# Rotary embedding and score matmul: the first batch in groups of eight heads, two row slots per step

## Chip, cores and metric

The kernel runs on one core of a Trainium2 chip. The metric is the device time of one execution in microseconds (us); the median of three runs before the change is 792.87 (792.67 to 793.26).

The engines of the core: TensorE (PE; its weight loads are shown as PEld) multiplies and transposes, VectorE (DVE) and ScalarE (ACT) work on elements and copy results out of the accumulator memory, GpSimd (POOL) and SyncE (SP) issue transfers. The transfers themselves run on 16 DMA engines.

## The reference

Sixteen batches, 512 rows, 16 heads of 64 elements, all float32. q and k are rotated by position, then for each row s every head h is multiplied with the same head of every row t; there is no scaling and no softmax.

```python
batch, seq, heads, dim = 16, 512, 16, 64
...
q_rot = concatenate([q1 * cos - q2 * sin, q1 * sin + q2 * cos], axis=-1)
k_rot = concatenate([k1 * cos - k2 * sin, k1 * sin + k2 * cos], axis=-1)
scores = np.einsum('bshd,bthd->bsht', q_rot, k_rot)
```

q and k are 33.6 MB each, the output is 268.4 MB.

## The kernel before

**Tiling.** The 512 rows of a batch are split into 128 partitions with C = 4 rows each: partition p holds rows 4p to 4p + 3, and the four places are called slots. A step i computes one slot of one batch for all 16 heads: i // 4 is the batch, i % 4 the slot, 64 steps in all. Each step has eight score steps p (`scores(i, p, st)`): one pair of heads each, two score matmuls of 64 x 128 by 64 x 512 into a score buffer `ps` (three buffers), and one copy by ScalarE (line 208) into the stage tile `st`, 128 partitions by 16 heads by 512. A full `st` is stored with one transfer of 4 MB, 32 KB in each partition.

**Rotation and transposes.** `rope` returns two lists of VectorE work, products (lines 149 and 150) and sums (line 154), on the loaded tile in place, with a scratch tile `part`. `transposed` turns four blocks of 128 x 128 into one bank `bank` (two buffers) by TensorE (line 170) and copies them with VectorE or ScalarE (line 185) into `qT` (two buffers) or `kT` (two buffers). `tr_act` does that for both halves, with ScalarE.

**The first batch** is done otherwise. Its q and k are cut by heads, not by slots: a unit n (0 to 3) is four heads of all 512 rows. The units are loaded into one tile `early`: first unit 0 of k and q (512 KB each), then units 1 to 3 in one transfer each (1536 KB each). `rope(which, n)` with n below 4 turns a unit; from 4 on, n names a slot of a later batch: `("k", 4)` is slot 0 of batch 1, `("q", 8)` would be slot 0 of batch 2. In the first batch step i computes unit i, that is four heads for all four slots: score step p has slot c = p // 2 and head pair hp = p % 2. After every second score step 1 MB is stored, four heads by 512 columns, 8 KB in each partition (line 211). Between the score steps stand, in each of the four steps, the next unit's rotation and transposes, and one slot of batch 1's k.

**Order.** All of it is under a hand-written schedule: each engine runs its instructions in the order in which the program issues them, and waits where an operand or a buffer is not ready. So an instruction that waits holds up all that is behind it on its engine. Stores and most loads are issued by SP, in order; a few loads later in the kernel go over GpSimd (`load_around`).

**Buffers.** The stage pool has three slots of 4 MB; `early` lies in one of them during the first batch. A step's `st` takes the slot of three steps before, and ScalarE's first copy into it waits until the stores from it have landed. By the trace step 2 takes the slot of step 0, step 3 that of `early`, step 4 that of step 1. Loaded tiles of later batches (`k_sb`, `q_sb`) have two buffers each; batch 1 and batch 2 fill them.

**The steady part** (line 264 on): in step i, q of step i + 1 is transposed after score steps 1 and 3 and copied by VectorE, k of the step four further after score steps 5 and 6 and copied by ScalarE; VectorE turns q two steps ahead and k five ahead.

Of the kernel before, what the change touches and what calls it, by code (L numbers as in the profile page):

```python
# [10 lines left out]
def kernel(  # L11
# [8 lines left out]
    nc = tc.nc  # L20
    fp32 = mybir.dt.float32
# [3 lines left out]
    B, S, H, D = q.shape  # L25
    HD = D // 2
    P = 128
    C = S // P
    HP = H // 2
    NST = B * C  # L30
    G = H // C
# [22 lines left out]

    st_first = [stage_pool.tile([P, H, S], fp32, tag="stage", name="st") for _ in range(2)]
    early = stage_pool.tile([P, 2 * C * H * D], fp32, tag="stage", name="early")
    units = {}
    used = [0]  # L60

# [51 lines left out]
    def load(which, b):  # L113

        if b >= B:
            return
        t = in_pool.tile([P, C, H * D], fp32, tag=which + "_in", name=which + "_sb")
        batches[which, b] = t
        if (which, b) in RELIEVED:
            load_around(which, b, t)  # L120
        else:
            nc.sync.dma_start(t.rearrange("p c (h d) -> p c h d", h=H), dram[which][b])
# [35 lines left out]
    kT = {}  # L158
    qT = {}

    def transposed(which, n, g, copy):


        bank = ps_t_pool.tile([P, 4, P], fp32, tag="ps_t", name="bank")
        for x in range(4):
            if n < C:
                src = units[which, n][:, x, P * g : P * (g + 1)]
            else:
                src = batches[which, n // C][:, n % C, P * (4 * g + x) : P * (4 * g + x + 1)]
            nc.tensor.transpose(bank[:, x, :], src, ident)  # L170
        src = bank
        if which == "q":
            if n not in qT:
                qT[n] = qt_pool.tile([P, HP, P], fp32, tag="qT", name="qT_t")
            dst = qT[n][:, 4 * g : 4 * g + 4, :]
        else:
            b = n // C
            if b not in kT:
                kT[b] = kt_pool.tile([P, HP, S], fp32, tag="kT", name="kT_t")
            if n < C:  # L180
                dst = kT[b][:, 2 * n + g].rearrange("p (t c) -> p t c", c=C)
                src = bank.rearrange("p c t -> p t c")
            else:
                dst = kT[b][:, 4 * g : 4 * g + 4, P * (n % C) : P * (n % C + 1)]
        copy(out=dst, in_=src)  # L185

    def store(i, st):
        nc.sync.dma_start(o_v[i // C, i % C], st)

    def scores(i, p, st):  # L190

        ps = ps_s_pool.tile([P, 2, S], fp32, tag="ps_s", name="ps")
        b = i // C
        if b == 0:
            c, hp = divmod(p, 2)
            lhs, rhs = qT[i][:, C * hp + c], kT[0][:, 2 * i + hp]
        else:
            lhs, rhs = qT[i][:, p], kT[b][:, p]
        for r in range(2):
            po, rh = ps[:, r, :], rhs[64 * r : 64 * r + 64, :]  # L200
            nc.tensor.matmul(  # L201
                out=po, lhsT=lhs[64 * r : 64 * r + 64, :], rhs=rh, start=True, stop=True
            )
        so, si = st[:, 2 * p : 2 * p + 2, :], ps
        if b > 0:
            so = so.rearrange("s r (t c) -> s r t c", c=C)
            si = si.rearrange("s r (c t) -> s r t c", c=C)
        nc.scalar.copy(out=so, in_=si)  # L208
        if b == 0 and p % 2 == 1:
            c = p // 2  # L210
            nc.sync.dma_start(o_v[0, c, :, G * i : G * (i + 1)], st[:, G * c : G * (c + 1)])
        elif b > 0 and p == HP - 1:
            store(i, st)

    def tr_act(which, n):
        for g in range(2):
            transposed(which, n, g, nc.scalar.copy)

    def run(ops):
        for op in ops:  # L220
            op()

    with tc.manual_schedule():
        for t, src in ((cos_t, cos), (sin_t, sin)):
            nc.scalar.dma_start(t, src.rearrange("(p c) j -> p c j", c=C))
        for head, heads in ((0, G), (G, H - G)):
            load_units("k", head, heads)
            load_units("q", head, heads)
        load("k", 1)
        load("q", 1)  # L230
        make_identity(nc, ident)
        nc.scalar.copy(out=ss_t[:, :, 0, :], in_=sin_t)
        nc.scalar.mul(ss_t[:, :, 1, :], sin_t, -1.0)
        for which in ("k", "q"):
            run(rope(which, 0))
            tr_act(which, 0)


        for i in range(C):
            st = st_first[i] if i < 2 else stage_pool.tile([P, H, S], fp32, tag="stage", name="st")  # L240
            if i < C - 1:
                dve = rope("k", i + 1) + rope("q", i + 1) + rope("k", C + i)
                nxt = [("k", i + 1), ("q", i + 1)]
            else:
                dve = rope("q", C) + rope("k", C + i) + rope("q", C + 1) + rope("k", 2 * C)
                nxt = [("q", C), ("k", C + i)]
            for p in range(HP):
                scores(i, p, st)
                if p in (0, 1) and i > 0:
                    run(dve[:1])  # L250
                    dve = dve[1:]
                    transposed("k", C + i - 1, p, nc.vector.tensor_copy)
                if p == 3 and i < 2:
                    load("kq"[i], 2)
                if p in (2, 6):
                    m = len(dve) - (4 if p == 2 else 2) - (2 if i == C - 1 else 0)
                    run(dve[:m])
                    dve = dve[m:]
                    tr_act(*nxt.pop(0))
            run(dve)  # L260
        load("k", 3)


        for i in range(C, NST):
            tr = {}
            if i + 1 < NST:
                tr[1], tr[3] = ("q", i + 1, 0), ("q", i + 1, 1)
            if i + C < NST:
                tr[5], tr[6] = ("k", i + C, 0), ("k", i + C, 1)
            dve = []  # L270
            if i + 2 < NST:
                dve += rope("q", i + 2)
            if i + 1 + C < NST:
                dve += rope("k", i + 1 + C)
            st = stage_pool.tile([P, H, S], fp32, tag="stage", name="st")
            for p in range(HP):
                scores(i, p, st)
                if p not in tr:
                    continue
                if tr[p][0] == "q":  # L280
                    run(dve[:1])
                    dve = dve[1:]
                    transposed(*tr[p], nc.vector.tensor_copy)
                else:
                    transposed(*tr[p], nc.scalar.copy)
            run(dve)
            if i % C == C - 2:
                load("q", i // C + 2)
            elif i % C == C - 1:
                load("k", i // C + 3)  # L290
# [30 lines left out]
```

## Time and profile before

| what | value |
|---|---|
| median of three runs | 792.87 us |
| profiled execution: first to last instruction (span) | 790.4 us |
| TensorE / VectorE / ScalarE / GpSimd busy | 684.4 / 544.7 / 562.0 / 11.9 us |
| DMA mean rate, bytes | 425 GB/s, 336.18 MB |
| share of SP's DMA queue in the 16 engines' span | 96.4% |
| stores of 4096 KB | 60, 24.7 us from issue to landing |
| stores of 1024 KB (first batch) | 16, 13.8 us from issue to landing |
| mean granted TensorE clock | 0.934 |

The profiled execution has no time of its own beside its span; the span is 2.5 us under the median of the runs.

How to read the profile: it shows one execution. Columns of a timeline are start (us from the span's start), duration, engine, line, operation, result and operand; in square brackets stands the idle time of the engine just before, and what ended it. "PEclk" is the granted TensorE clock. "x3" merges three instructions. A window lists the busy time of each engine with its number of instructions, and at the end the clock, the DMA engines' mean busy share and GB/s. The trace also holds a record of each DMA packet (queue, size, start, duration) and of each landing, where each of the 16 DMA engines raises a semaphore by one.

The first transfers are issued in this order, by the SP queue's timeline: the four loads of units at 0.74, 1.46, 2.11 and 2.78, batch 1's k at 3.45 and q at 4.17, the first two stores at 19.52 and 22.46, batch 2's k at 22.85, further stores, batch 2's q at 33.73, the sixteenth store at 62.29, batch 3's k at 62.72.

### The profile page before, as it was taken

How to read it: one execution, taken by the hardware profiler on the slowest of the kernel's cores; microseconds unless marked ns; L12 is line 12 of the kernel's file. 1: busy time of each engine (PE TensorE's matmuls, PEld its weight loads, DVE VectorE, ACT ScalarE, POOL GpSimd, SP SyncE). 2: the span in 40 equal slices, each digit the busy share in tenths (PEclk: the TensorE clock that was granted, in tenths of full speed). 3: DMA queues.
4: the chain of work that ended last, by engine and by line, in shares of the span. 5: the costliest groups of instructions: out<-in, count | busy, mean ns of one | idle time of the engine just before them, and what ended most of it. 6: DMA issues, size and time to landing. Idle time of an engine off the chain costs nothing.

```text
span 790.4 us, 7750 instructions
## 1 busy us (share of the span) xinstructions
PE 684.4 (87%) x3072; PEld 296.4 (38%) x3072; DVE 544.7 (69%) x516; ACT 562.0 (71%) x647; POOL 11.9 (2%) x24
## 2 busy tenths in 40 slices
PE   4989998988988889798996989889899798799960
PEld 2444443433433334343342433334334343344420
DVE  6999988666766678576785767667678487587400
ACT  3888886865857768486785866777577586588770
POOL 0000000000001000000000001000000000000000
PEclk9999999998999999898998989999899899899995
DMA  9999999999999999999999999999999999999997
GB/s 357 417 425 439 429 430 435 425 435 436 429 429 428 413 432 419 433 423 438 433 427 436 426 432 429 422 432 424 430 432 427 436 429 432 430 432 434 432 429 340
DMA packets 18836, 336.18 MB, mean 425 GB/s; under 512 B 2312, under 2 KB 3592, under 8 KB 4616
## 3 DMA queue, kind: packets, MB, share of 16 engines
q1 hardware_dynamic: 16704, 325.46, 96.4%
q0 software_dynamic: 1808, 10.10, 3.1%
q8 instruction: 24, 0.39, 0.2%
q10 hardware_dynamic: 288, 0.13, 0.1%
q14 instruction: 12, 0.10, 0.0%
HBM read 67.24 MB, written 268.44 MB: 425 GB/s over the span
## 4 chain that ended last, share of the span: by engine, by line
DMA 49%; PE 40%; ACT 5%; DVE 3%; issue 1%; ACTq 0%; SPq 0%; DVEq 0%
DMA out_dram<-st 46%; PE ps L201 30%; PE bank L170 10%; ACT st L208 5%; DMA q_sb<-in_q_dram 2%; DVE part L149 1%; DMA early<-in_k_dram 1%; DVE q_sb L150 0%; DVE k_sb L154 0%; DVE k_sb L150 0%; DVE q_sb L154 0%; DVE early L150 0%; DVE kT_t L185 0%; ACTq L316 0%; DVE early L154 0%
## 5 line engine op out<-in xcount | busy, mean ns | idle before, releaser
L208 ACT COPY st<-ps 128x1024 f32<-128x1024 f32 x512 | 495.7, 1020 | 192.6 <-DMA out_dram<-st 109.8
L201 PE MATMUL ps<-kT_t,qT_t 64*128 64x512 f32 x2048 | 544.0, 649 | 67.0 <-ACT st L208 67.0
L201 PEld LDWEIGHTS ps<-kT_t,qT_t 64*128 64x128 f32 x2048 | 183.6, 196 | 256.2 <-issue 133.3
L185 DVE COPY qT_t<-bank 128x512 f32<-128x512 f32 x118 | 81.6, 691 | 193.9 <-PE bank L170 193.9
L170 PEld LDWEIGHTS bank<-ident,q_sb 128*128 128x128 f32 x480 | 54.2, 149 | 99.0 <-issue 96.4
L170 PEld LDWEIGHTS bank<-ident,k_sb 128*128 128x128 f32 x480 | 50.3, 140 | 96.4 <-DVE k_sb L150 39.5
L170 PE MATMUL bank<-ident,q_sb 128*128 128x128 f32 x480 | 85.1, 304 | 0.9 <-PE ps L201 0.9
L170 PE MATMUL bank<-ident,k_sb 128*128 128x128 f32 x480 | 78.5, 286 | 1.6 <-DVE qT_t L185 1.2
L185 ACT COPY kT_t<-bank 128x512 f32<-128x512 f32 x122 | 72.4, 598 | 6.4 <-PE bank L170 6.4
L154 DVE TENSOR_TENSOR k_sb<-k_sb,part 128x1024 f32<-128x1024 f32 x60 | 73.5, 1225 | 2.1
L150 DVE TENSOR_TENSOR q_sb<-q_sb,cos_t 128x1024 f32<-128x1024 f32 x60 | 73.5, 1225 | 2.1
L150 DVE TENSOR_TENSOR k_sb<-k_sb,cos_t 128x1024 f32<-128x1024 f32 x60 | 73.5, 1225 | 2.0
L149 DVE TENSOR_TENSOR part<-q_sb,ss_t 128x1024 f32<-128x1024 f32 x60 | 73.5, 1225 | 2.0
L149 DVE TENSOR_TENSOR part<-k_sb,ss_t 128x1024 f32<-128x1024 f32 x60 | 73.0, 1216 | 0.9 <-DMA k_sb<-in_k_dram 0.7
L154 DVE TENSOR_TENSOR q_sb<-q_sb,part 128x1024 f32<-128x1024 f32 x60 | 72.9, 1216 | 0.0
L170 PE MATMUL bank<-ident,early 128*128 128x128 f32 x64 | 10.5, 315 | 12.4 <-DVE early L154 10.5
L170 PEld LDWEIGHTS bank<-ident,early 128*128 128x128 f32 x64 | 8.3, 161 | 17.4 <-issue 13.4
L149 DVE TENSOR_TENSOR part<-early,ss_t 128x1024 f32<-128x1024 f32 x8 | 9.8, 1222 | 5.8 <-DMA early<-in_k_dram 5.7
L98 POOL DMA_DIRECT2D q_sb<-in_q_dram x3 | 2.3, 752 | 620.2 <-PE bank L170 446.2
L154 DVE TENSOR_TENSOR early<-early,part 128x512 f32<-128x512 f32 x16 | 10.3, 687 | 0.2
L150 DVE TENSOR_TENSOR early<-early,cos_t 128x1024 f32<-128x1024 f32 x8 | 9.8, 1225 | 0.3
L185 ACT COPY qT_t<-bank 128x512 f32<-128x512 f32 x10 | 5.7, 629 | 3.2 <-PE bank L170 3.2
(12 smaller groups left out, 15.9 us busy)
## 6 DMA issues: line engine op xcount, KB each, us to landing
out_dram<-st SPq DMA_DIRECT2D x60, 4096.0 KB, 24.7
k_sb<-in_k_dram SPq DMA_DIRECT2D x13, 2048.0 KB, 28.3
q_sb<-in_q_dram SPq DMA_DIRECT2D x12, 2048.0 KB, 26.5
out_dram<-st SPq DMA_DIRECT2D x16, 1024.0 KB, 13.8
q_sb<-in_q_dram POOLq DMA_DIRECT2D x3, 1920.0 KB, 27.8
k_sb<-in_k_dram POOLq DMA_DIRECT2D x2, 1920.0 KB, 43.3
early<-in_k_dram SPq DMA_DIRECT2D x1, 1536.0 KB
early<-in_q_dram SPq DMA_DIRECT2D x1, 1536.0 KB
```

Source lines behind the costliest of these rows:

```text
L98: nc.gpsimd.dma_start(dst, src)
L149: nc.vector.tensor_tensor(pv, xs, ss, op=mult)
L150: nc.vector.tensor_tensor(xc, xc, cs, op=mult)
L154: nc.vector.tensor_tensor(y, y, z, op=add)
L170: nc.tensor.transpose(bank[:, x, :], src, ident)
L185: copy(out=dst, in_=src)
L201: nc.tensor.matmul(out=po, lhsT=lhs[64 * r : 64 * r + 64, :], rhs=rh, start=True, stop=True)
L208: nc.scalar.copy(out=so, in_=si)
```

## The change

Only the first batch is done in another order. A step i now computes two units (eight heads) for two slots: steps 0 and 1 take units 0 and 1 with slots 0, 1 and then 2, 3; steps 2 and 3 take units 2 and 3 likewise (`order`). Within a step the four score steps of the first unit come before the four of the second. A store is issued after score steps 5 and 7: eight heads by 512 columns of one slot, 2 MB, 16 KB in each partition; eight stores in place of sixteen. Batch 2's k is loaded ahead of all stores, right behind batch 1's loads, and batch 2's q after step 0. A table (`plan`) says after which score step which rotation, transpose or load is issued: VectorE turns units 0 to 3 of k and q one after the other, then batch 1's k slots 0 and 1, whose transposes it copies behind score steps 6 and 7 of step 2, and so on. In the list, "rope" is a rotation, "act" the transposes with ScalarE's copies, "dve" one half of a slot's transposes with VectorE's copy. `early` is allocated between the two first stage tiles. The steady part is as it was.

```diff
--- before.py
+++ after.py
@@ -54,8 +54,9 @@
 
 
 
-    st_first = [stage_pool.tile([P, H, S], fp32, tag="stage", name="st") for _ in range(2)]
+    st_first = [stage_pool.tile([P, H, S], fp32, tag="stage", name="st")]
     early = stage_pool.tile([P, 2 * C * H * D], fp32, tag="stage", name="early")
+    st_first.append(stage_pool.tile([P, H, S], fp32, tag="stage", name="st"))
     units = {}
     used = [0]
 
@@ -187,28 +188,37 @@
     def store(i, st):
         nc.sync.dma_start(o_v[i // C, i % C], st)
 
+    E8 = 2 * G
+    order = [
+        [(2 * (i // 2) + u, 2 * (i % 2) + c, hp) for u in range(2) for c in range(2) for hp in range(2)]
+        for i in range(C)
+    ]
+
     def scores(i, p, st):
 
         ps = ps_s_pool.tile([P, 2, S], fp32, tag="ps_s", name="ps")
         b = i // C
         if b == 0:
-            c, hp = divmod(p, 2)
-            lhs, rhs = qT[i][:, C * hp + c], kT[0][:, 2 * i + hp]
-        else:
-            lhs, rhs = qT[i][:, p], kT[b][:, p]
+            u, c, hp = order[i][p]
+            lhs, rhs = qT[u][:, C * hp + c], kT[0][:, 2 * u + hp]
+            at = E8 * (c % 2) + G * (u % 2) + 2 * hp
+        else:
+            lhs, rhs, at = qT[i][:, p], kT[b][:, p], 2 * p
         for r in range(2):
             po, rh = ps[:, r, :], rhs[64 * r : 64 * r + 64, :]
             nc.tensor.matmul(
                 out=po, lhsT=lhs[64 * r : 64 * r + 64, :], rhs=rh, start=True, stop=True
             )
-        so, si = st[:, 2 * p : 2 * p + 2, :], ps
+        so, si = st[:, at : at + 2, :], ps
         if b > 0:
             so = so.rearrange("s r (t c) -> s r t c", c=C)
             si = si.rearrange("s r (c t) -> s r t c", c=C)
         nc.scalar.copy(out=so, in_=si)
-        if b == 0 and p % 2 == 1:
-            c = p // 2
-            nc.sync.dma_start(o_v[0, c, :, G * i : G * (i + 1)], st[:, G * c : G * (c + 1)])
+        if b == 0 and u % 2 == 1 and hp == 1:
+            g = i // 2
+            nc.sync.dma_start(
+                o_v[0, c, :, E8 * g : E8 * (g + 1)], st[:, E8 * (c % 2) : E8 * (c % 2 + 1)]
+            )
         elif b > 0 and p == HP - 1:
             store(i, st)
 
@@ -228,6 +238,7 @@
             load_units("q", head, heads)
         load("k", 1)
         load("q", 1)
+        load("k", 2)
         make_identity(nc, ident)
         nc.scalar.copy(out=ss_t[:, :, 0, :], in_=sin_t)
         nc.scalar.mul(ss_t[:, :, 1, :], sin_t, -1.0)
@@ -236,28 +247,38 @@
             tr_act(which, 0)
 
 
+        plan = {
+            (0, 3): [
+                ("rope", "k", 1), ("act", "k", 1), ("rope", "q", 1), ("act", "q", 1),
+                ("rope", "k", 2), ("rope", "q", 2),
+            ],
+            (0, 7): [("load", "q", 2)],
+            (1, 2): [("act", "k", 2), ("rope", "k", 3), ("rope", "q", 3)],
+            (1, 6): [("act", "q", 2), ("rope", "k", C), ("rope", "k", C + 1)],
+            (2, 1): [("act", "k", 3)],
+            (2, 2): [("act", "q", 3)],
+            (2, 6): [("dve", "k", C, 0)],
+            (2, 7): [("dve", "k", C, 1), ("rope", "k", C + 2)],
+            (3, 1): [("dve", "k", C + 1, 0)],
+            (3, 2): [("dve", "k", C + 1, 1), ("rope", "q", C)],
+            (3, 4): [("dve", "k", C + 2, 0)],
+            (3, 5): [("dve", "k", C + 2, 1), ("rope", "k", C + 3)],
+            (3, 6): [("act", "q", C)],
+            (3, 7): [("act", "k", C + 3), ("rope", "q", C + 1), ("rope", "k", 2 * C)],
+        }
         for i in range(C):
             st = st_first[i] if i < 2 else stage_pool.tile([P, H, S], fp32, tag="stage", name="st")
-            if i < C - 1:
-                dve = rope("k", i + 1) + rope("q", i + 1) + rope("k", C + i)
-                nxt = [("k", i + 1), ("q", i + 1)]
-            else:
-                dve = rope("q", C) + rope("k", C + i) + rope("q", C + 1) + rope("k", 2 * C)
-                nxt = [("q", C), ("k", C + i)]
             for p in range(HP):
                 scores(i, p, st)
-                if p in (0, 1) and i > 0:
-                    run(dve[:1])
-                    dve = dve[1:]
-                    transposed("k", C + i - 1, p, nc.vector.tensor_copy)
-                if p == 3 and i < 2:
-                    load("kq"[i], 2)
-                if p in (2, 6):
-                    m = len(dve) - (4 if p == 2 else 2) - (2 if i == C - 1 else 0)
-                    run(dve[:m])
-                    dve = dve[m:]
-                    tr_act(*nxt.pop(0))
-            run(dve)
+                for what, which, n, *g in plan.get((i, p), ()):
+                    if what == "rope":
+                        run(rope(which, n))
+                    elif what == "load":
+                        load(which, n)
+                    elif what == "act":
+                        tr_act(which, n)
+                    else:
+                        transposed(which, n, g[0], nc.vector.tensor_copy)
         load("k", 3)
```

## The prediction

> **What bounds the kernel now.** I read the 40 slices and the table of DMA queues first.
>
> ```profile
> DMA  9999999999999999999999999999999999999997
> q1 hardware_dynamic: 16704, 325.46, 96.4%
> ```
>
> The 16 DMA engines are full in every slice but the last, while no compute engine is over 87%. So a microsecond in which they stand empty is lost for good, and one of packets that falls away is won. The windows say the same of the first 100 us.
>
> ```profile
> core 0: us, PE busy (x) PEld busy (x) DVE busy (x) ACT busy (x) POOL busy (x), PEclk, DMA share, GB/s
> 20.00:40.00 20.00, 20.00 (x105) 9.48 (x103) 19.40 (x21) 16.65 (x22) 0.00 (x0) 1.00 1.00 419
> 40.00:60.00 20.00, 17.91 (x93) 8.59 (x92) 19.62 (x22) 16.85 (x21) 0.00 (x0) 1.00 1.01 425
> 60.00:76.00 16.00, 14.75 (x72) 6.56 (x72) 15.66 (x15) 12.87 (x16) 0.00 (x0) 1.00 1.02 433
> ```
>
> But VectorE (DVE) is 97 to 98% busy here too: the first batch is where a second resource is nearly full. So I looked, in the timelines of ScalarE, VectorE and the SP queue, at what would make it late.
>
> ```profile
> 36.97 1.01 ACT L208 COPY st<-ps 128x1024 f32<-128x1024 f32 x1
> 40.59 1.93 ACT L208 COPY st<-ps 128x1024 f32<-128x1024 f32 x2 [2.61 <-DMA out_dram<-st]
> ...
> 44.85 1.29 DVE L154 TENSOR_TENSOR early<-early,part 128x512 f32<-128x512 f32 x2
> 46.18 1.22 DVE L149 TENSOR_TENSOR part<-k_sb,ss_t 128x1024 f32<-128x1024 f32 x1
> ...
> 66.02 1.23 DVE L149 TENSOR_TENSOR part<-q_sb,ss_t 128x1024 f32<-128x1024 f32 x1
> 67.27 1.23 DVE L150 TENSOR_TENSOR q_sb<-q_sb,cos_t 128x1024 f32<-128x1024 f32 x1
> 68.42 0.68 DVE L185 COPY qT_t<-bank 128x512 f32<-128x512 f32 x1
> ...
> 72.65 2.84 ACT L208 COPY st<-ps 128x1024 f32<-128x1024 f32 x3 [0.23 <-PE ps L201]
> ...
> 73.69 0.33 SPq L188 DMA_DIRECT2D out_dram<-st  x1
> ...
> 83.71 0.33 SPq L188 DMA_DIRECT2D out_dram<-st  x1
> ```
>
> The first two rows: step i = 2 writes into the stage slot of i = 0 and ScalarE stands until that slot's stores have landed (the last landing of the fourth is at 40.49 in the trace). VectorE does not feel it: it always has rotations queued that need nothing of that step, and from 5.67 to 66.02 its rows leave one hole, of 0.19. The last rows: q's products of i = 4, the copy at 68.42, and 5.27 us after its start the first 4 MB store, at 73.69. The next follows 10.02 later.
>
> How thin the DMA's reserve is there: the packet records of the trace have the first 32 KB packet, with which the first engine begins that store, at 77.3. From issue to first packet it takes 1.46 on SP's idle queue (issue at 0.74, packet at 2.2) and 0.96 on ScalarE's (0.74 to 1.7). So the store could have come only 77.3 - 73.69 - 1.46 = 2.15 us later before an engine ran dry.
>
> **The change, part by part.** *Packets.* Sixteen stores of 1 MB become eight of 2 MB. By the packet records an 8 KB packet takes 309 ns, a 16 KB one 611, the 4-byte packet that closes a store on each engine 9. Each engine had 16 x 8 = 128 of 8 KB and now has 64 of 16 KB: 64 x (618 - 611) = 0.45 us, and 8 x 9 = 0.07 for the closings: -0.52 us in all. [...]
>
> *The start.* VectorE turns k0, q0, k1, q1 in this order already, so q1 is done at 21.03 as now. The first store now needs six score steps and both units. Of TensorE and ScalarE I count from the rows of now: third score copy at 19.39, fourth 20.30, two bank copies of k1 (0.48 apart) to 22.3, q1's transposes once the two banks are free, its copies to 23.65, score steps five and six, whose copies end at 25.4 and 26.3. Store at 26.3 where the first was at 19.52; data at 27.8. The engines have k's load of batch 2 more to do by then: in the records the first 8 KB packet starts at 23.5, plus 8 x 0.611 = 4.9, gives 28.4. So no pause, by 0.6 us. That load and q's of batch 2 only change places with stores; both land long before their use. All later 2 MB stores of the batch (34.6, 37.5, about 48, 50, 58, 62.5 by the same counting) meet a queue that is 3 to 5 us ahead.
>
> *Step i = 2.* Its slot is again that of i = 0, whose two stores end where the four ended: 28.4 + 9.8 = 38.2 for the first engine against 38.3 now, so ScalarE starts at 40.5 again. What is queued behind it differs. VectorE, which waits for nothing, finishes k0 to k3 and q0 to q3 (8 rotations of 3.84 us, the distance from 5.67 to 9.52 in its timeline), then batch 1's slots 0 and 1 (3.78 each, 21.06 to 24.84): 5.67 + 30.72 + 7.56 = 43.95. Its next instruction is the copy of slot 0's transposes, and these stand on TensorE behind score step (2,6). That step needs the score buffer of (2,3), one of three, so ScalarE must first do 3 score copies at 0.905, two pairs of bank copies at 1.03 and the copy of (2,3), 1.01: 40.5 + 2.7 + 2.1 + 1.0 = 46.3. TensorE then takes 0.95 to the transposes and VectorE starts 0.69 after them (26.82 to 27.51 now): 47.9. **VectorE stands 4.0 us**, and about 1.0 more until the second half comes at 49.6, after (2,7). The list of work it has to do before q's products of i = 4 is the same as now, so these slip from 66.02 by 4.0 + 1.0 - 0.2 = 4.8; adding up each row from 49.6 on gives 5.2. I take 5.0. TensorE and ScalarE cannot catch up: i = 3's last scores, i = 4's first and its k banks wait on exactly these VectorE rows (two transpose banks, both held until VectorE copies).
>
> *The first 4 MB store* then goes out at 73.69 + 5.0 = 78.7, its data at 80.15. The engines are dry from 76.8 (77.3 less the 0.52) on the first one. The 16 landings of the load before it are spread from 77.68 to 79.92, eight of them within 0.3 of the first; so the last engine runs dry at about 79.0. Against now the first engine starts the store 80.15 - 77.3 = 2.85 later, the last one 80.15 - 79.5 = 0.65 later. The kernel ends with the last engine; six of the 16 end within 1.3 us of it in the records, and half of the engines belong to the early ones, so I take 2.5. From here the compute makes a 4 MB store every 10.02 us (TensorE is 20.00 of 20 busy at 80 to 100) and an engine needs 8 x 1.213 = 9.7 for it: two more pauses of 0.3, until q's load behind the third store refills the queue. With engines that were late I count 0.5. Then loads lift the DMA's demand to 4 x 9.7 + 2 x 4.9 = 48.6 per four steps against 40 of TensorE, and nothing later is late.
>
> *Nothing else.* As many matmuls, transposes, copies and rotations as now. k's load of batch 3 goes from 62.7 to about 65, still 7 us ahead of the engines. The `early` tile's slot goes to i = 3 in both (the copy at 49.81 now waits for no store), and is free earlier.
>
> **Sum.** Span 790.4 + 2.5 + 0.5 = 793.4 (the 0.52 is inside the 2.5). The median lies 2.5 above the profiled span; so **795.9 us**, +0.4%. Bounds of the unknowns: the last finisher was an early engine, +2.85 and +0.6, or a late one, +0.65 and +0.3; VectorE's slip 4.8 to 5.2; latency 0.96 to 1.46, and for a large store perhaps 0.5 more than that: +0.4 to +4.2 together, 793.3 to 797.1.
>
> **Rivals.** *The start runs dry as well.* If the store at 26.3 is over 0.6 us late, the engines stop at 28.4, the two stores of i = 0 land as much later, and i = 2, VectorE and the 4 MB store slip by it too. For it: a margin of 0.6 on a chain of a dozen rows. Against: every row of it is measured in the same place. Two us late: the store at 78.7 + 1.4, the end at about 797.3; decides from 0.6 us on.
>
> *Not slower: step i = 2 waits only for the store of the half it writes.* Its first copies write half of the slot, which the first store empties at 33.3 plus some 2 to land. Then ScalarE goes on at 37.5, all of i = 2 comes 3.0 earlier, VectorE stands 1 to 2 us instead of 5, the 4 MB store goes out at 75.7 and its data at 77.2 meets engines dry from 76.8: the loss is about 0.4 less the 0.5 of packets, +0.3 for the later pauses: 793.1. It decides if the wait ends before 38. For it: a region that is free. Against: the wait row at 40.59 ends with the last of four stores though its copy wrote the first quarter.
>
> *The last finisher was one of the late engines:* 0.65 + 0.3, 793.8; the pause is there but eats only the lead of the others.
>
> **Chances.** What a measurement of this kernel can tell from no change is about 0.2%, 1.6 us. Forecast 0.68, start dry too 0.14, late finisher 0.05, not slower 0.13. Of the last, 0.03 fall below 791.3 and 0.10 within; the late finisher is within. Slower 0.82, same 0.15, faster 0.03. The range goes from 793.4 to 798.6, the upper end for the dry start with a late large store.
>
> **What would show it.** Right: a wait of ScalarE that still ends near 40.5; a hole of about 4 us in VectorE's rows near 44 to 48, before a copy of kT_t, put down to TensorE; the first 4 MB store near 78.7; a DMA share well under 1 near 77 to 80, and 8 stores of 2048 KB. Wrong: no hole in VectorE, the 4 MB store before 76, or a full DMA row in all the first 100 us; or a gap near 28, which would be the first rival.

## The result and the profile after

| | before | after |
|---|---|---|
| median on the same chip | 792.77 us (792.47 to 793.26, 4 runs) | 799.74 us (798.08 to 800.24, 4 runs) |
| ratio, 95% interval | | 1.0082 (1.0069 to 1.0095) |
| profiled execution: time, span | span 790.4 us | 799.78 us, span 798.0 us |

The change makes the kernel 7.0 us slower; 3.0 were forecast, and 799.74 lies 1.1 above the top of the range. The kernel of after ran once more beside the experiments: 798.77 us against 793.77, 1.0064 (1.0048 to 1.0079). So the loss is 5 to 7 us.

The page of after: the DMA row and the GB/s row of its 40 slices, the queue of SP, and one row of the DMA issues.

```profile
DMA  9998999999999999999999999999999999999996
GB/s 353 432 423 377 420 395 425 434 422 440 428 430 431 411 430 413 436 423 437 433 431 432 426 435 427 426 429 408 428 436 424 443 426 429 430 438 430 434 430 298
q1 hardware_dynamic: 15552, 325.46, 95.8%
out_dram<-st SPq DMA_DIRECT2D x8, 2048.0 KB, 12.3
```

The packets of SP's queue are 1152 fewer, 1024 data packets and 128 closing ones (the 4-byte packet that ends a store on each engine), as worked out. The DMA row, full before, has an 8 in the slice of 60 to 80 us. GB/s shows a second low place that the DMA row does not: 395 in the sixth slice (100 to 120), where the engines count as busy. There lies about half of the loss that was not forecast.

ScalarE, VectorE and the SP queue around step 2, from the timelines of after:

```profile
36.24 1.16 ACT L216 COPY st<-ps 128x1024 f32<-128x1024 f32 x1
40.45 1.93 ACT L216 COPY st<-ps 128x1024 f32<-128x1024 f32 x2 [3.05 <-DMA out_dram<-st]
...
42.60 1.23 DVE L155 TENSOR_TENSOR k_sb<-k_sb,part 128x1024 f32<-128x1024 f32 x1
48.33 0.69 DVE L186 COPY kT_t<-bank 128x512 f32<-128x512 f32 x1 [4.50 <-PE bank L171]
49.98 0.69 DVE L186 COPY kT_t<-bank 128x512 f32<-128x512 f32 x1 [0.95 <-PE bank L171]
...
79.28 20.37 SPq L189 DMA_DIRECT2D out_dram<-st  x3
```

This is the forecast chain, link by link: ScalarE's wait ends at 40.45 (40.5 was said), VectorE's last rotation ends at 43.83 (43.95), it stands 4.50 (4.0) and 0.95 (1.0), and the first 4 MB store is issued at 79.28 (78.7); the row merges three stores, 10.02 apart.

Now the same three windows of both kernels: the pause, the two stores behind it, and the stretch with q's load of batch 3. The last two columns are the DMA engines' mean busy share and GB/s.

```profile
core 0: us, PE busy (x) PEld busy (x) DVE busy (x) ACT busy (x) POOL busy (x), PEclk, DMA share, GB/s
76.00:84.00 8.00, 8.00 (x40) 3.32 (x36) 7.90 (x8) 7.17 (x9) 0.00 (x0) 1.00 1.04 446
84.00:104.00 20.00, 20.00 (x98) 8.85 (x96) 18.13 (x18) 17.34 (x21) 0.00 (x0) 1.00 1.00 430
104.00:122.00 18.00, 18.00 (x88) 8.08 (x88) 15.10 (x16) 15.49 (x18) 0.00 (x0) 1.00 1.00 431
```

That was before; after:

```profile
76.00:84.00 8.00, 7.98 (x42) 3.62 (x40) 7.86 (x8) 6.35 (x8) 0.00 (x0) 1.00 0.78 334
84.00:104.00 20.00, 20.00 (x100) 8.82 (x98) 18.16 (x19) 17.38 (x20) 0.00 (x0) 1.00 0.98 419
104.00:122.00 18.00, 18.00 (x90) 7.87 (x86) 15.74 (x15) 15.77 (x19) 0.00 (x0) 1.00 0.99 380
```

Line 1 is the pause: a share of 0.78. Line 2 is the thin stretch, 0.98. Line 3 is the surprise: a share of 0.99, and yet 380 GB/s where 431 flowed before. The engines are not idle there, their packets are slow.

The packet records tell which. Between 104 and 122, of 16 KB packets (q's load) and of 32 KB packets (the stores), those more than 0.1 us over the usual 0.611 and 1.213 (called long); and what all packets together took over the usual, divided by 16 engines (the **added packet time** from here on):

```
kernel   16 KB packets: long of all, mean of a long one   32 KB: long of all, mean   added, us per engine
before     0 of 144                                         1 of 164   1.593          0.05
after     44 of 128   1.061                                16 of 144   1.921          2.01
```

In after 15 long 32 KB packets start at 108.7 or 108.8, nearly one on each engine, and long packets of the load follow until 116.3.

**Where 7.6 us of span went.** The mean engine closes its last store at 792.36 instead of 786.62, +5.74: pauses of 3.1 (2.48 between 70 and 84, 0.55 between 84 and 110, 0.08 later), packets saved -0.52, longer packets +2.94 (5.30 to 8.24 over the whole execution; 1.96 of it in the stretch just shown), and 0.2 of the start. The last engine is now 3.79 behind the mean one and was 2.38: +1.41. From the last closing to the end of the span it is 1.85 instead of 1.36: +0.49. Together 7.64. The last two terms, 1.9 of it, are those of one execution: in after again the last engine is 2.14 behind the mean one, less than in before, and the mean engine closes at 794.29 instead; over the profiles of all runs the last engine is 2.1 to 4.1 behind.

### The profile page after: what moved, and what is told of

It is laid out like the page before. It is cut to its first block, busy times and chain, and to the rows that moved or that the text cites. A ratio compares the mean times of both kernels' runs of the same rounds, so it can differ in the third digit from the quotient of the medians.

```text
span 798.0 us, 7730 instructions
## 1 busy us (share of the span) xinstructions
PE 686.6 (86%) x3072; PEld 297.2 (37%) x3072; DVE 544.9 (68%) x516; ACT 562.3 (70%) x647; POOL 11.9 (1%) x24
## 4 chain that ended last, share of the span: by engine, by line
DMA 47%; PE 40%; ACT 6%; DVE 3%; issue 1%; ACTq 0%
DMA out_dram<-st 47%; PE ps L209 30%; PE bank L171 10%; ACT st L216 5%; DVE part L150 1%; DMA sin_t<-in_sin_dram 0%; DVE k_sb L151 0%; DVE k_sb L155 0%; DVE kT_t L186 0%; DVE q_sb L151 0%; DVE q_sb L155 0%; ACT kT_t L186 0%; DVE early L151 0%; ACTq L337 0%; DVE early L155 0%
## 5 line engine op out<-in xcount | busy, mean ns | idle before, releaser
L171 PE MATMUL bank<-ident,q_sb 128*128 128x128 f32 x480 | 86.7, 308 | 0.5 <-DVE kT_t L186 0.5
```

## The experiments

The theory had two halves: the pause, and a stretch of long packets that the pause brings about. The rivals: that the long packets come from the new order of the first batch whatever the pause does; that a start which ran late in some executions, not the hole, decides; that long packets come of engines which the pause has lined up, so that all turn from writing to reading at once. All runs in one table; pause is that of the mean engine between 70 and 110 us, and "T4" is the issue of the first 4 MB store (of the first half of it in halves). Median and range are of all runs; T4, pause and added packet time are of one profiled execution, which need not be the median one.

```
run           median (range), runs          before   ratio (95%)               T4      pause  added 104-122
no hole       795.60 (793.41-798.90), 12    793.42   1.0032 (1.0019-1.0044)    75.23   0.00   1.16
halves        794.24 (793.65-797.32), 10    793.42   1.0013 (1.0003-1.0023)    73.14   0.00   0.09
late x3       796.92 (796.04-798.97), 4     793.42   1.0045 (1.0032-1.0058)    77.91   1.30   1.96
late x4       798.48 (797.63-799.69), 4     793.42   1.0062 (1.0049-1.0075)    78.71   2.00   1.98
safe start    794.43 (793.81-796.92), 11    793.77   1.0014 (1.0005-1.0024)    76.84   0.97   1.81
safe + hole   798.49 (797.69-799.80), 4     793.77   1.0060 (1.0044-1.0075)    79.20   3.03   1.96
stagger       803.72 (802.85-805.45), 4     793.77   1.0128 (1.0113-1.0142)    80.81   4.39   1.74
after again   798.77 (797.80-800.12), 4     793.77   1.0064 (1.0048-1.0079)    80.70   2.90   2.01
filled        794.30 (792.55-796.23), 12    793.62   1.0007 (0.9998-1.0017)    76.23   0.11   1.75
load later    799.89 (799.10-800.13), 4     793.62   1.0078 (1.0065-1.0091)    81.12   5.04   0.80
late x2       795.53 (793.93-796.90), 10    793.96   1.0023 (1.0013-1.0033)    75.84   0.01   1.53
late x6       801.08 (800.97-802.06), 4     793.96   1.0093 (1.0077-1.0109)    81.86   2.80   2.06
```

**No hole.** The changed kernel, with a third slot's rotation ahead of the place where VectorE stood; the later rotations each move up one place.

```diff
-            (1, 6): [("act", "q", 2), ("rope", "k", C), ("rope", "k", C + 1)],
+            (1, 6): [("act", "q", 2), ("rope", "k", C), ("rope", "k", C + 1), ("rope", "k", C + 2)],
-            (2, 7): [("dve", "k", C, 1), ("rope", "k", C + 2)],
+            (2, 7): [("dve", "k", C, 1), ("rope", "q", C)],
-            (3, 2): [("dve", "k", C + 1, 1), ("rope", "q", C)],
+            (3, 2): [("dve", "k", C + 1, 1), ("rope", "k", C + 3)],
-            (3, 5): [("dve", "k", C + 2, 1), ("rope", "k", C + 3)],
+            (3, 5): [("dve", "k", C + 2, 1)],
```

> The changed kernel, with batch 1's third k slot turned before VectorE's hole in place of behind it, and each later rotation one place earlier. Theory 1, the pause and what it brings: all of the loss comes from VectorE's hole of 4.5 us at 43.8 and the pause of the DMA engines at 77 to 80 that follows; without it the first 4 MB store goes out near 75.5 instead of 79.3, its first packet comes at 76.3 before the engines are dry at 77.1, and the time is that of before less 0.5 for the packets: 792.3, within 791.8 to 793.2. Theory 2, something else in the change costs the 3.9 us that the forecast missed (the 16 KB stores, their order with the loads): the pause goes but these stay, 796 or so.

Measured: 795.60 against 793.42. Its timelines of VectorE and SP, then the third window:

```profile
48.06 0.69 DVE L186 COPY kT_t<-bank 128x512 f32<-128x512 f32 x1 [0.60 <-PE bank L171]
75.23 0.33 SPq L189 DMA_DIRECT2D out_dram<-st  x1
```

```profile
104.00:122.00 18.00, 18.00 (x89) 7.94 (x86) 15.13 (x15) 15.43 (x19) 0.00 (x0) 1.00 0.99 397
```

The hole shrinks from 4.50 to 0.60, the store comes 4.05 earlier than in after, there is no pause in this execution, and with one rotation moved ahead (and the later ones up) the loss falls from 5.0 to 7.0 us to 2.2. That VectorE's list and not the grouping itself made the delay is shown. But 2.2 us stay in the median, and the third window still reads 397. The profiled execution took 793.87, the second shortest of twelve: that the slower ones, up to 798.90, had no pause is not shown.

**Halves.** The changed kernel, hole and all; only batch 1's four stores go out in two halves of 2 MB, after score steps 3 and 7.

```diff
+        elif b == 1 and p % 4 == 3:
+            h = E8 * (p // 4)
+            nc.sync.dma_start(o_v[b, i % C, :, h : h + E8], st[:, h : h + E8])
-        elif b > 0 and p == HP - 1:
+        elif b > 1 and p == HP - 1:
             store(i, st)
```

> The changed kernel, with the four stores of batch 1 issued in two halves of 2 MB, after score steps 3 and 7; VectorE's hole stays. Theory 1: the hole costs only by way of the DMA pause. The first half goes out near 72.9, so the engines never stop; 792.3 to 793.5. Theory 2: VectorE's late start itself costs, whatever the stores do: 797 to 800.

Measured: 794.24 against 793.42. Two windows:

```profile
36.00:46.00 10.00, 8.14 (x46) 4.28 (x47) 8.57 (x8) 7.90 (x13) 0.00 (x0) 1.00 1.00 346
104.00:122.00 18.00, 18.00 (x88) 7.98 (x88) 15.74 (x15) 15.83 (x19) 0.00 (x0) 1.00 1.01 430
```

The engines get work before the reserve is used up, at 73.14, and neither the pause nor the slow stretch follows: 430 GB/s. So the first rival falls: the long packets are not a property of the new order. As the stores of this stretch have 16 KB packets here, not 32, this rests on the next two runs as well. The first window shows the same slowness elsewhere, 346 at a share of 1.00: in this execution the first store went out at 28.07, too late for the reserve that was to last to 28.4, and after a pause of 0.32 q's load of batch 2 had the long packets (added 2.03 between 30 and 60; 0.29 in after, whose start had no pause).

**Late x3 and x4.** The kernel before, with VectorE made late by repeating one product of batch 1's slot 2; the result is the same. A repeat is 1.22 us. Nothing of the change is in these.

```diff
-            nc.vector.tensor_tensor(pv, xs, ss, op=mult)
+            for _ in range(4 if (which, n) == ("k", C + 2) else 1):
+                nc.vector.tensor_tensor(pv, xs, ss, op=mult)
```

> The kernel before, in which VectorE repeats one product of batch 1's third k slot three times more (3 x 1.26 = 3.8 us of added work at 46, the same result). The first 4 MB store goes out at 77.5, first packet at 78.3; engines run dry between 77.3 and 79.6, half of them by 77.6. If only the pause counts: 0.7 on the mean engine and two of 0.3 after it, 793.8 to 794.4. If a pause also lines the engines up and their later packets take longer (2.9 us on the mean engine in the changed kernel): some of that comes on top, 795 to 797.

> The kernel before, with four repeats of that product (5.0 us of added VectorE work at 46, the same result), nothing of the change in it. The first 4 MB store goes out at 78.7, first packet at 79.5; a pause of 2.0 on the mean engine and two of 0.3. Only the pause counts: 795.2 to 795.8. The pause lines the 16 engines up and later packets take longer: as slow as the changed kernel, 798 to 800. The loss is not VectorE's at all: 792.8.

Measured: 796.92 and 798.48 against 793.42. The windows of the second:

```profile
76.00:84.00 8.00, 8.00 (x40) 3.61 (x40) 7.86 (x8) 6.67 (x8) 0.00 (x0) 1.00 0.84 363
104.00:122.00 18.00, 18.00 (x87) 7.91 (x86) 15.60 (x15) 15.92 (x19) 0.00 (x0) 1.00 1.00 385
```

A delay of VectorE alone, in the old order, makes both halves of the loss: the 4 MB store at 78.71, a share of 0.84 at the pause, and 385 GB/s thirty us later.

**The start.** Its own part was to be told apart by storing step 0 in four pieces of 1 MB, so that the first store goes out near 20 and no dry start can come: once without the hole, once with it, beside the kernel of after again.

```diff
+        if i == 0 and hp == 1:
+            nc.sync.dma_start(o_v[0, c, :, G * u : G * (u + 1)], st[:, at - 2 : at + 2])
-        if b == 0 and u % 2 == 1 and hp == 1:
+        elif b == 0 and u % 2 == 1 and hp == 1:
```

Safe start and no hole (with the edit of the first experiment):

> The changed kernel without VectorE's hole (as in e1) and with the first step's stores in four of 1 MB, one after every second score step, so the first goes out near 19.5 in place of 26.3. e1's times spread over 5.5 us though its profile shows no pause. Theory A: in many executions the start is later than in the profile, the first store misses the queue's end at 28.4, and the engines pause and line up there; with the early store the spread closes to that of the kernel before and the time is that of before less 0.26 for the packets. Theory B: the spread has another cause (loads that meet 16 KB stores): the median stays 2 us above before.

Safe start with the hole (otherwise the kernel of after):

> The changed kernel with VectorE's hole left in and only the first step's stores in four of 1 MB. Theory A: what is left is the pause at 77 to 80 (3.0 us on the mean engine), longer packets behind it (1.9) and the 0.26 gained: about 4.5 to 5 above before, some 2 below the changed kernel. Theory B: as slow as the changed kernel.

The kernel of after again:

> The changed kernel once more, on the chip of the other three, so that they have it beside them. Theory A: its first store comes at 26.3 to 28.5 from run to run, and the runs lie between 798 and 802. If the start were never late: 797 to 798 as the pause and the long packets alone give.

Measured: 794.43, 798.49 and 798.77 against 793.77. The same window of 36 to 46 in the last two, first safe start with the hole, then after again, whose first store was issued at 27.18:

```profile
36.00:46.00 10.00, 8.32 (x44) 4.02 (x44) 7.77 (x7) 8.07 (x13) 0.00 (x0) 1.00 1.03 436
```

```profile
36.00:46.00 10.00, 8.24 (x37) 4.27 (x38) 7.98 (x8) 7.12 (x11) 0.00 (x0) 0.85 1.00 359
```

The late start is there in after again and costs packets (359 instead of 436 GB/s), but the two medians are 0.3 apart, within each other's ranges. So the start is a real second weakness of the change, and not what decides its time; the hole does: 794.43 without it and 798.49 with it at the same safe start, 4.1 us. Without the hole the start does count: no hole is 2.2 above its before, safe start 0.7 (other chips, and the intervals of the two ratios just overlap).

Safe start did not get its whole gain. In its profile ScalarE shows a wait on TensorE a few us behind the slot wait:

```profile
46.49 1.93 ACT L216 COPY st<-ps 128x1024 f32<-128x1024 f32 x2 [1.43 <-PE ps L209]
```

TensorE's granted clock was 0.5 for 3.4 us from 43.0 on, so its score matmuls took longer; the 4 MB store came at 76.84, not 75.2, and the reserve of 2.15 was used up.

**Stagger.** If the lined-up engines are the cause of the long packets, setting them apart should cure it. Behind the first 4 MB store four tiny loads were put, on a different number of partitions each, to give the engines unequal work.

```diff
+                if i == C and p == HP - 1:
+                    lo = 0
+                    for n in (28, 20, 6, 3):
+                        src = bass.AP(q.tensor, 0, [(512, n), (2, 48), (1, 1)])
+                        dst = scratch[lo : lo + n, 48:96].rearrange("p (a b) -> p a b", b=1)
+                        nc.sync.dma_start(dst, src)
+                        lo += n
```

> The changed kernel with four tiny loads into a spare tile behind the first 4 MB store, of 48 four-byte packets in each of 28, 20, 6 and 3 partitions, which keep some engines longer than others: up to 2.6 us more on three of them, 1.5 on the mean. Theory, the engines that are lined up take longer for the load of batch 3's q at 110 to 117 (1.9 us of added packet time on the mean engine at 105 to 120 in the changed kernel): it falls under 0.6, and the time is about the changed kernel's (-1.3 + 1.5) or 1 more. Rival, the long packets have nothing to do with the line-up: still 1.5 to 2.2, and the time 1.5 to 2.6 above the changed kernel's.

Measured: 803.72. The edit did something else than meant, as SP's queue shows:

```profile
80.81 0.33 SPq L189 DMA_DIRECT2D out_dram<-st  x1
81.19 12.79 SPq L304 DMA_DIRECT2D scratch<-in_q_dram  x4
94.09 0.37 SPq L189 DMA_DIRECT2D out_dram<-st  x1
```

The four issues took until 94, and the next store stood behind them and came 13.28 after the first instead of 10.02. The queue ran dry a second time and the engines were in line again (their closings of that second store lie between 104.68 and 104.82). So it is no test of setting them apart. It shows something else: the third store, issued at 100.84, got its first packet only at 104.68, so the queue was well ahead again (3.84 us; 2.95 in before), and still 1.74 us of added packet time came.

**Filled.** Safe start, and VectorE's list written anew so that rotations stand wherever it waited for TensorE ("prod" and "sum" are the first and the second half of a rotation).

```diff
+            (1, 6): [("act", "q", 2), ("rope", "k", C), ("rope", "k", C + 1), ("rope", "k", C + 2)],
...
+            (2, 6): [("prod", "q", C), ("dve", "k", C, 0)],
+            (2, 7): [("sum", "q", C), ("dve", "k", C, 1), ("prod", "k", C + 3)],
+            (3, 1): [("dve", "k", C + 1, 0), ("sum", "k", C + 3)],
+            (3, 2): [("dve", "k", C + 1, 1)],
+            (3, 4): [("dve", "k", C + 2, 0)],
+            (3, 5): [("dve", "k", C + 2, 1), ("rope", "q", C + 1)],
+            (3, 6): [("act", "q", C)],
+            (3, 7): [("act", "k", C + 3), ("rope", "k", 2 * C)],
```

> The changed kernel with both repairs: the first step's stores in four of 1 MB, and VectorE's list reordered so that a rotation or half of one always stands between its copies (batch 1's third k slot before the hole, q's products and sums split around the copies). The first 4 MB store should go out at 73.5 to 75, as before, so that a TensorE clock that is granted late at the start (17.6 to 20.4 in the traces so far) or lost at 43 no longer empties the DMA queue. Theory (all of the loss is pauses and the long packets behind them): no pause in the trace, added packet time at 104 to 122 under 0.3, median 0 to 0.5 below before on the same chip, spread of the runs as before's. Rival (8-head groups and 2 MB stores cost by themselves): 1 to 2 above before.

Measured: 794.30 against 793.62, a ratio of 1.0007 (0.9998 to 1.0017): no difference that can be told. It takes back nearly all of the loss, and does not beat the kernel before; none of the runs does. Its 4 MB store came at 76.23, again with a granted clock of 0.5 for a while from 44.5, and the third window is slow though the pause was 0.11; the added packet time is 1.75, where no pause and under 0.3 were expected:

```profile
104.00:122.00 18.00, 18.00 (x87) 7.86 (x86) 15.09 (x16) 15.43 (x18) 0.00 (x0) 1.00 1.00 389
```

**Load later.** Is the slow stretch bound to a time after the pause, or to the load? Safe start with the hole, and q's load of batch 3 issued one step later, behind the fourth 4 MB store and next to k's.

```diff
-            if i % C == C - 2:
+            if i % C == C - 2 and i > 2 * C:
...
+                if i < 2 * C:
+                    load("q", i // C + 2)
```

> The changed kernel with the first step's stores of 1 MB, VectorE's hole left in, and the load of batch 3's q moved one step later, behind the fourth 4 MB store. It asks what the long packets behind the pause hang on. The first load behind a pause is long wherever it stands: 1 to 2 us of added packet time on the mean engine move with it, to 120 to 127. They belong to the time right after the pause: at 104 to 122 as before, in the stores, and little at 120 to 127. They need the engines in line and these drift apart in 10 us: under 0.5 in both. Time 798 to 799.5 in the first two cases, 797 in the third; one more pause of 0.3 in all.

Measured: 799.89, 1.4 above the 798.49 of safe start with the hole (another chip). Its windows:

```profile
104.00:122.00 18.00, 18.00 (x88) 8.01 (x87) 15.50 (x15) 15.86 (x20) 0.00 (x0) 1.00 1.00 411
122.00:142.00 20.00, 20.00 (x98) 8.82 (x97) 17.09 (x16) 16.53 (x20) 0.00 (x0) 1.00 1.01 413
```

No 32 KB packet is long before 119.3 here (in after they begin at 108.7); 17 are from there to 122.0, and then 39 of 256 load packets until 133.4, most of them in k's load, few in q's that goes ahead of it. The added packet time is 0.80 before 122 and 0.98 from 122 to 142. So the long packets go with the switch from stores to loads and move with the load; but which packets of a load they take is not explained.

**Late x2 and x6.** How much must the queue thin, and does the price grow with the pause?

> The kernel before with two repeats of the product (2.5 us of added VectorE work at 46, the same result). The first 4 MB store goes out at 76.2, first packet at 77.0, just ahead of the first engine's end at 77.3: no pause where TensorE's clock stays, the time that of before. If instead VectorE's lateness costs as such: 2.5 above. If a thin queue is enough for the long packets: no pause in the trace but 1 to 2 us of added packet time at 104 to 122, 1 to 2 above before.

> The kernel before with six repeats (7.6 us of added VectorE work, the same result). The first 4 MB store goes out at 81.2. If the cost is a step for the long packets (about 2) and the pause's own length on top: 2.5 above late4, that is 7 to 8 above before, with 4.0 of pause at 77 to 82, two of 0.3, and again 1.7 to 2.1 of added packet time at 104 to 122. If the long packets grow with the pause: over 3 of them, 9 or more above before.

Measured: 795.53 and 801.08 against 793.96. The issue of the first 4 MB store and two windows of late x2, then the same windows of late x6:

```profile
75.84 0.33 SPq L189 DMA_DIRECT2D out_dram<-st  x1
```

```profile
76.00:84.00 8.00, 8.00 (x42) 3.65 (x40) 7.86 (x9) 6.82 (x8) 0.00 (x0) 1.00 1.03 444
104.00:122.00 18.00, 18.00 (x88) 7.83 (x84) 15.11 (x15) 15.43 (x19) 0.00 (x0) 1.00 1.02 401
```

```profile
76.00:84.00 8.00, 7.35 (x38) 3.15 (x36) 7.86 (x9) 6.75 (x8) 0.00 (x0) 1.00 0.83 350
104.00:122.00 18.00, 18.00 (x90) 7.94 (x86) 15.71 (x15) 15.64 (x19) 0.00 (x0) 1.00 1.01 386
```

The first has its store 2.15 later than before, just the reserve that the prediction worked out, and no engine pauses: a share of 1.03. Yet 401 GB/s follow, 1.53 us of added packet time. (This execution, 793.93, is the shortest of its ten; its span is 792.1 against the 790.4 of before's profile.) Late x6 pauses 1.35 between 24 and 70 and 2.80 between 70 and 110, and its slow stretch is no worse than that of late x4, 2.06 against 1.98. Ordered by the time from the issue of the third 4 MB store (the last before the load; its second half in halves) to its first packet, with stagger apart:

```
kernel                         issue to first packet    added packet time 104-122
before                         2.95 us                  0.05
halves                         3.5                      0.09
no hole                        1.2                      1.16
late x2                        0.8                      1.53
filled                         0.6 to 0.8               1.75
dry (safe start, late x3 and
x4, after, safe + hole, x6)    0.5 to 0.8               1.81 to 2.06
stagger                        3.84                     1.74
```

A store on an empty queue shows 0.5 to 0.8 between the two. So in all but stagger the price is nearly a step: it comes when the queue has next to nothing ahead of it, even if no engine has stopped yet, and is about 2 us however long the pause is. Against before, the medians of the four late kernels are 1.6 us longer at no pause, 3.5 at 1.30, 5.1 at 2.00, 7.1 at 4.15: about 1.6 for the thin queue and 1.3 to 1.75 for each us of pause (5.5 / 4.15 to 3.5 / 2.00); why a us of pause costs more than one is not shown. After, with 3.1 of pauses and 0.52 of packets saved, would be by this at +5.1 to +6.5; measured were +7.0 and +5.0. The rule is rough, and two runs do not keep it: safe start would be at +2.5 or more and filled at +1.4, with 0.39 of packets saved in each (six of the eight 2 MB stores are left; 0.26 was expected), and both medians are at +0.7. Their profiled executions, 795.03 and 794.64, lie above these medians.

## Why the prediction fell short

**Right: the chain to the store.** The wait of ScalarE, what queues behind it on TensorE, VectorE's two holes, and the slip of q's products up to the 4 MB store all came within 0.6 us of the forecast. That it is this chain is shown by the pair at the safe start: without the hole 4.1 us are gone. The late kernels show the reverse: a delay of VectorE at the same place in the old order costs 1.6 to 7.1.

**Right: packets and pause.** -0.52 for packets is what the records have. Of the sum's 2.5 + 0.5 = 3.0, the pauses less the packets make 2.6. Part of this is luck, as two errors cancel in it: the store was issued 0.6 later than said, in an execution whose TensorE clock was 0.5 for 3.4 us from 65.5 on, and its first packet came 0.82 after the issue, not 1.46. The 0.5 more that the bounds allowed for a large store is shown by no run; on an empty queue the large stores had 0.5 to 0.8.

**Wrong: "nothing later is late".** This is the step that failed. The sum let the loss end when q's load had refilled the queue, taking a packet to cost what it always costs. Just there, at the switch from the third store to that load, the packets were longer: 1.96 us on the mean engine between 104 and 122, of 2.94 in the whole execution. The late kernels show that the delay brings this price without anything of the change, and late x2 that it comes without a pause: 1.53 of added packets, a profiled span 1.8 longer than before's and a median 1.6 longer. The step counted idle time of engines only. In before the same stretch has 0.05, but long packets stand elsewhere in it (1.70 us between 230 and 330, 5.30 in all); the sum gave them no term.

**Wrong in size: the last finisher, in this execution.** The step took the last engine to lose no more than the first, 2.5 between 0.65 and 2.85. In the profile of after it went the other way: the last engine is 3.79 behind the mean one, not 2.38, so +1.41 came on top. What is short adds up: 2.94 + 1.41 + 0.49 (closing to end of the span) + 0.2 = 5.0, and 2.6 + 5.0 = 7.6. In after again the 1.41 is -0.24, and the mean engine is 7.67 later, not 5.74, with more long packets at the start as well; so this term is scatter between executions more than a price of the change. The step from span to median gave 0.76 back: 2.5 was taken from a profile that was itself below the median, and after's median lies 1.74 above its span.

**The rivals.** The dry start was given 0.14 with a margin of 0.6; that margin was no larger than what the start varies by. In the first profile of after the store went out at 26.31, as forecast (26.3), and there was no pause; in after again at 27.18 and in halves at 28.07 it was late, and the long packets followed (1.70 and 2.03 between 30 and 60). Behind the hole its price is masked, since safe start with the hole ran as long as after again. The late finisher, 793.8, did not come: the last engine fell further behind. The slot that comes free by halves, 793.1, did not come either: the wait ended at 40.45 with the last store.

**Open: why the packets lengthen.** That they come at the switch from stores to loads after a late first 4 MB store, and move with the load, is shown. The cause is not, and the records rule out two simple ones. It takes no engines in line: in no hole and late x2 the 16 engines close the second store over 2.75 and 2.59 us (2.31 in before), and long packets follow. And it takes no thin queue at the third store: in stagger the queue is 3.84 ahead there, with the engines in line, and 1.74 follow. Only before and halves have neither, and they have none. In load later the second load has more long packets than the first. Long packets stand elsewhere too (in before 5.30 us in all, 0.05 of it between 104 and 122), and those were not looked into.

## What to carry to other kernels

On a kernel bound by its transfers, follow each wait for a stage slot to the in-order list of the engine that works beside it, and put work there that needs nothing of the step that waits: one rotation moved ahead of a transpose copy, and the later ones up, was worth 4.1 us here. Keep more queued than just avoids a pause: with 3 us from a store's issue to its first packet 430 to 431 GB/s flowed in the stretch with the next load (before, halves), with 1.2 or less 378 to 401, in no hole and late x2 though no engine had paused; that cost about 1.6 us here. (Stagger, with its engines in line after the second pause, is the exception.) The bytes per second show it while the busy share does not (431 at 1.00 in before, 380 at 0.99 in after). A margin of 0.6 us at the start is none when the start itself moves by 0.9 and more.

## What the runs showed of the chip

**The clock of TensorE changes at other times in each run.** In the first profile of after the score matmuls take 0.59 us from 17.82 on and 0.94 to 1.22 before; in after again they take 0.59 from 19.55, in halves from 20.49. The first store moves with that, 26.31, 27.18, 28.07 (VectorE's first product also began later, at 5.54, 5.89 and 6.48). Later the clock falls again for a while, in other places in each execution. The timelines of TensorE around step 2, first of after, then of after again:

```profile
38.99 1.13 PE L209 MATMUL ps<-kT_t,qT_t 64*128 64x512 f32 x4
42.92 1.15 PE L171 MATMUL bank<-ident,early 128*128 128x128 f32 x8 [2.80 <-ACT kT_t L186]
```

```profile
39.87 1.13 PE L209 MATMUL ps<-kT_t,qT_t 64*128 64x512 f32 x4
42.76 1.74 PE L171 MATMUL bank<-ident,early 128*128 128x128 f32 x8 [1.75 <-ACT kT_t L186]
```

TensorE idles 2.80 us in the first, and its eight transposes still take 1.15; it idles 1.75 in the second, and they take 1.74. The records of the granted clock (start, how long, clock) show why:

```
after         17.73  47.79  1.0 |  65.51  3.41  0.5 |  68.93  75.09  1.0
after again   19.15  23.89  1.0 |  43.04  3.41  0.5 |  46.45  20.48  1.0 |  66.93  3.41  0.5
```

From 43.04 on the transposes of after again ran at 0.5, those of after ran at 1.0 throughout. Every length in the two rows is a whole multiple of 3.413 us to within 0.01: 14, 1, 22, and 7, 1, 6, 1. What makes the clock fall is not shown. Between 36 and 46 us its mean was 0.85 in after again and in safe start, 0.88 in load later and 0.93 in filled, where TensorE idled 1.75, 1.86, 1.98 and 2.91 us ahead of these transposes; it was 1.00 in safe start with the hole, halves and after, where it idled 1.68, 1.86 and 2.80. So the length of this idle time alone does not tell.

Between the two executions of after, with the full clock from 17.73 and from 19.15, the first store moved by 0.9 us (up to 0.35 of it from VectorE's later start), and the margin of the start was 0.6.

**A window can be full and slow.** A DMA share of 1.00 or a little over went with 346 to 446 GB/s in the windows above. The median packet stays at 611 to 681 ns (16 KB) and 1213 ns (32 KB) in all of them; the long ones have means of 884 to 1138 and 1593 to 1960.
